# Recurrent unit of a hybrid backbone: branch products two tiles ahead, each convolution behind the gates of the tile in front

## The chip, the cores and the metric

The kernel runs on one core of a Trainium2 chip. Its five engines work side by side, each through its own queue in order: PE (TensorE, matrix products), ACT (ScalarE, functions), DVE (VectorE, elementwise work and scans), POOL (GpSimd) and SP (which here only issues DMAs). They wait for each other by semaphores. The metric is the time of one execution in microseconds (us), as the device measures it; the median of three runs is given.

## The reference

One inference step runs two trunk layers over 512 latent and 128 context tokens of width 1024. Layer 0 mixes tokens by neighbourhood attention, layer 1 by a bidirectional gated linear recurrent unit; behind each stands a SwiGLU feed-forward part. The change lies in layer 1's mixer:

```
def _rglru_coeffs(xc, w_a, b_a, w_i, b_i, lam):
    xb = xc.reshape(B, T, LRU_BLOCKS, LRU_BLOCK_W)
    r = sigmoid(einsum('btnk,nkj->btnj', xb, w_a).reshape(B, T, D) + b_a)
    i = sigmoid(einsum('btnk,nkj->btnj', xb, w_i).reshape(B, T, D) + b_i)
    log_a = -LRU_C * r * softplus(-lam)
    a = exp(log_a)
    b = sqrt(-expm1(2.0 * log_a)) * (i * xc)

def _lru_mixer(xm, h0, w_in, conv_w, conv_b, ...):
    gate, xr = jnp.split(xm @ w_in, 2, axis=-1)
    xc = _centred_depthwise_conv(xr, conv_w, conv_b)     # width 4
    # coefficients a, b for each direction; h_t = a_t * h_(t-1) + b_t
    y = (hs_f + hs_b) * gelu(gate)
    return y @ w_out, ...
```

Everything is float32.

## The kernel before

Tokens lie along the free dimension (640 columns: 512 latent, 128 context), features along the 128 partitions, so that a width of 1024 is eight tiles. Products with the large weights are done as three matmuls in a faster float format: weights and activations are each split into a high and a low part, and `some` (L214) multiplies high by high, high by low and low by high. A weight tile of 1024 x 128 is a unit: `unit` (L163) loads it twice in this stage, once by SP into `raw` (L167) and once by POOL straight into the high part `whi` (L178); DVE then makes the low part `wlo` as raw minus whi (L182). There are three buffers each of raw, whi and wlo.

The recurrent unit treats the eight tiles of its width one by one, in steps of the loop at L1438:

- `lru_xr` (L1242): the branch product of tile f, 24 matmuls (eight feature tiles, three each) over the first 384 columns and 24 over the other 256, copied by ACT (L1251) into `xr`. Two xr buffers.
- `lru_a` (L1254): loads the four 128 x 128 gate weights `gw` (SP, L1257); the convolution, one ACT step (L1259) and three DVE steps (L1261), into `xc`, two buffers; then four gate products (L1271, four float32 matmul records each) into `gp`, a PSUM tile with two buffers, each followed by a tanh on ACT (L1272); last a DVE step on the second pair (L1273), the last reader of xc.
- `lru_b` (L1276): coefficients; exp (L1283), tanh (L1284) and square root (L1285) on ACT, four DVE steps.
- `lru_c` (L1290): four scans and sums on DVE; POOL copies the last state of each direction (L1298).
- `lru_gate` (L1317): the product of the gate branch with its GELU (L1325, L1327).
- `lru_d` (L1307): the result times the gate, split for the output projection (L1313, L1315).

In step t of the loop the program asks for `lru_a` of tile t, the branch product of tile t+1, `lru_b` of tile t-1, `lru_c` of tile t-2, the gate branch of tile t-2 and `lru_d` of tile t-2. Ahead of the loop stand the branch products of tile 0 and half of tile 1 and the gate branch of tile 0, interleaved with the end of the stage before. The order in the program isn't the order on the engines: the kernel is built with a planner (`schedule_with_timeline_sim=True`, L1484) that lays the instructions into the five queues by a simulated timeline, with the program's order as the priority among those that are ready there. At run time each queue is in order.

Behind the unit comes the output projection (`project_halves`, L1463), which multiplies the first six tiles of its input in one pass and the last two in a second, and the last feed-forward part.

Of the kernel before, what the change touches and what calls it, by code (L numbers as in the profile page):

```python
# [9 lines left out]
F32 = mybir.dt.float32  # L10
# [5 lines left out]
P = 128  # L16
D = 1024
KT = D // P
# [15 lines left out]
LW = 643  # L34
# [91 lines left out]
class _Step:  # L126
# [1113 lines left out]
        return [lambda t0=t0, t1=t1, **kw: ev(t0, self.chunk(u, hi, lo, t0, t1, **kw)) for t0, t1 in CHL]  # L1240

    def lru_xr(self, f, hi, lo, after=None):  # L1242
        xr = self.xrs[f % 2]
        nat = xr[:, 2:514].rearrange("p (r c) -> p c r", r=ROWS)

        def ev(t0, ps):
            for o, a, b, r in ((nat[:, 56:64], 0, 64, ROWS), (nat[:, 0:40], 64, 384, ROWS),
                               (nat[:, 40:56], 384, 512, ROWS), (xr[:, 517:645], 512, 640, 0)):
                if t0 <= a and b <= t0 + 384:
                    v = ps[:, a - t0:b - t0]  # L1250
                    self.nc.scalar.copy(o, v.rearrange("p (c r) -> p c r", r=r) if r else v)  # L1251
        return self.halves(self.i["wi"][KT + f], hi, lo, ev, after)

    def lru_a(self, f, lp):  # L1254
        nc, xr = self.nc, self.xrs[f % 2]
        gw = self.t([P, 2, 2, P], F32, "gw", 2, lp)
        nc.sync.dma_start(gw, self.i["wg"][f])  # L1257
        xc = self.t([P, LW], F32, "xc", 2, lp)
        nc.scalar.activation(xc, xr[:, 0:LW], AF.Identity, scale=self.col("cw0", f), bias=self.col("cb", f))  # L1259
        for j in range(1, 4):  # L1260
            nc.vector.scalar_tensor_tensor(xc, xr[:, j:j + LW], self.col(f"cw{j}", f), xc, ALU.mult, ALU.add)  # L1261

        def lt():
            return self.t([P, 2, LW], F32, "lt", NLT, lp)
        tr, ti = lt(), lt()
        for w, tl in enumerate((tr, ti)):
            for d in range(2):
                c = (w * 2 + d) * KT + f
                ps = self.pp.tile([P, 1024], F32, tag="gp", name=self.nm("gp"), bufs=2)
                for s0, s1 in ((0, 512), (512, LW)):  # L1270
                    nc.tensor.matmul(ps[:, s0:s1], gw[:, w, d], xc[:, s0:s1], start=True, stop=True)  # L1271
                nc.scalar.activation(tl[:, d], ps[:, 0:LW], AF.Tanh, scale=0.5, bias=self.hb[:, c:c + 1])  # L1272
        nc.vector.scalar_tensor_tensor(ti, ti, 1.0, xc[:, None, :].broadcast_to([P, 2, LW]), ALU.add, ALU.mult)  # L1273
        return lt, tr, ti
# [63 lines left out]
    def run(self):  # L1338
        nc, tc, i, o = self.nc, self.tc, self.i, self.o
# [19 lines left out]
        xhi = self.big()  # L1359
        xlo = self.big()  # L1360
# [44 lines left out]
        xhi = self.big(n=NTOK + 2)  # L1405
        xlo = self.big(n=NTOK + 2)
# [12 lines left out]
        xhi, xlo = self.nh, self.nl  # L1419
# [2 lines left out]
        ylo = self.big()  # L1422
        with self.phase("lru", at=1) as lp:
            A, B, C, G = {}, {}, {}, {}
            self.xrs = [self.t([P, 648], F32, f"xr{j}", 1, lp) for j in range(2)]
            for xr in self.xrs:
                for a, b in ((0, 2), (514, 517), (645, 648)):
                    nc.gpsimd.memset(xr[:, a:b], 0.0)

            def gate(g, after=None):  # L1430
                G[g], halves = self.lru_gate(g, xhi, xlo, lp, after)
                return halves
            x0, g0, x1 = self.lru_xr(0, xhi, xlo), gate(0, self.sq), self.lru_xr(1, xhi, xlo, self.dg)
            x0[0](pins={3: self.at})
            g0[0](pins={0: self.rr})
            for step in (x1[0], x0[1], g0[1]):
                step()
            for t in range(KT + 2):  # L1438
                if t < KT:
                    A[t] = self.lru_a(t, lp)  # L1440
                if t + 1 < KT:
                    for step in self.lru_xr(t + 1, xhi, xlo) if t else x1[1:]:
                        step()
                if 0 < t <= KT:
                    B[t - 1] = self.lru_b(t - 1, *A.pop(t - 1))
                if t > 1:
                    C[t - 2] = self.lru_c(t - 2, *B.pop(t - 2))
                if t > 2:
                    for step in gate(t - 2):
                        step()  # L1450
                if t > 1:
                    self.lru_d(t - 2, C.pop(t - 2), G.pop(t - 2), yhi, ylo)
            nc.gpsimd.dma_start(o["nh"], self.st)
        x1, x2 = self.big(n=NTOK + 2), self.big(n=NTOK + 2)
# [33 lines left out]
```

## Time and profile before

| what | us |
|---|---|
| median of three runs | 1521.86 |
| lowest, highest | 1520.55, 1522.31 |
| the profiled execution | 1522.37 |
| its span in the profile | 1520.6 |
| gate products' matmuls (L1271) in the unit | from 875.29 to 991.3 |

The profile is of one execution. A timeline row gives an instruction's start, its length, its engine and line, what it writes and reads, and in brackets how long its engine had been idle and which instruction it waited for by the profile. An instruction that waits for several others is put down to the one that came last by the profile. Matmuls overlap in PE's pipeline, so the distance between two starts says more than a length. A row of windows gives the busy time of each engine in a stretch.

### The profile page before, as it was taken

To read this page: it belongs to the slowest core of one execution; us is meant where nothing else is said; L and a number is where in the kernel's file an instruction comes from. 1 tells how busy PE (TensorE), PEld (TensorE's weight loads), DVE (VectorE), ACT (ScalarE), POOL (GpSimd) and SP (SyncE) were. 2 spreads that over 40 slices of the span, in tenths; PEclk is the share of its full clock that TensorE was granted. 3 is DMA by queue.
4 is the path that set the end of the run, shared out by engine and by line. 5 is a ranking of instruction groups with operands and counts; after the bars stand their busy time and mean duration, and the time that the engine had idled before them with its cause. 6 is when DMAs were issued, how large, how long until landed. Compare 5 with 4: busy or idle time off the path is not lost. (4 is left out here: it accounts for less than half of the span.)

```text
span 1520.6 us, 26116 instructions
## 1 busy us (share of the span) xinstructions
PE 1491.2 (98%) x10373; PEld 1441.8 (95%) x10373; DVE 1061.5 (70%) x2005; ACT 698.1 (46%) x1268; POOL 261.4 (17%) x276
## 2 busy tenths in 40 slices
PE   8999999999999999999999999899999999999997
PEld 5999999889999999999999887799999999999997
DVE  5778998679999997434443769876975655566555
ACT  4676766654332123312321478764644342434243
POOL 0112132100111110000000014230232323222211
PEclk9999999999999999999999999999999999999999
DMA  9644665446556664222222543316242231323211
GB/s 375 174 143 160 186 189 167 117 139 194 176 185 195 207 196 132 62 84 84 65 73 83 150 134 102 119 59 216 70 156 80 74 111 57 100 67 97 71 56 70
DMA packets 72330, 196.65 MB, mean 129 GB/s; under 512 B 8048, under 2 KB 24592, under 8 KB 72080
## 3 DMA queue, kind: packets, MB, share of 16 engines
q1 hardware_dynamic: 57392, 142.32, 29.6%
q0 software_dynamic: 14240, 51.98, 11.1%
q8 instruction: 81, 1.33, 0.4%
q10 hardware_dynamic: 576, 0.68, 0.1%
q14 instruction: 41, 0.34, 0.1%
HBM read 179.48 MB, written 8.92 MB: 124 GB/s over the span
## 5 line engine op out<-in xcount | busy, mean ns | idle before, releaser
L221 PE MATMUL mm<-big,whi 128*128 128x320 f32 (+3 forms) x1233 | 383.9, 313 | 4.0 <-ACT big L1313 2.8
L222 PE MATMUL mm<-big,whi 128*128 128x320 f32 (+3 forms) x1233 | 384.2, 312 | 1.7 <-DVE big L1315 1.3
L223 PE MATMUL mm<-big,wlo 128*128 128x320 f32 (+3 forms) x1233 | 384.1, 312 | 0.2 <-DVE wlo L182 0.2
L221 PEld LDWEIGHTS mm<-big,whi 128*128 128x128 f32 x1233 | 233.0, 189 | 6.7 <-ACT big L1313 3.5
L222 PEld LDWEIGHTS mm<-big,whi 128*128 128x128 f32 x1233 | 233.6, 189 | 3.8 <-DVE big L1315 2.2
L223 PEld LDWEIGHTS mm<-big,wlo 128*128 128x128 f32 x1233 | 233.2, 189 | 1.6 <-DVE wlo L182 0.4
L250 DVE SCALAR_TENSOR_TENSOR mprod<-mraw,csb 128x1024 f32<-128x1024 f32 x160 | 194.9, 1218 | 11.8 <-DMA mraw<-in_wm 11.4
L590 DVE SCALAR_TENSOR_TENSOR x<-mm,G,x 128x320 f32<-128x320 f32 (+2 forms) x192 | 77.8, 435 | 82.4 <-PE mm L223 82.3
L180 ACT CAST whi<-raw 128x1024 fp32r<-128x1024 f32 (+1 forms) x71 | 73.9, 1041 | 113.9 <-PE mm L222 65.6
L182 DVE TENSOR_TENSOR wlo<-raw,whi 128x1024 fp32r<-128x1024 f32 (+1 forms) x87 | 105.9, 1218 | 28.7 <-ACT whi L180 16.5
L221 PE MATMUL mm<-big,whx 128*128 128x320 f32 (+3 forms) x348 | 108.4, 311 | 0.0
L223 PE MATMUL mm<-big,wlx 128*128 128x320 f32 (+3 forms) x348 | 108.0, 310 | 0.0
L222 PE MATMUL mm<-big,whx 128*128 128x320 f32 (+3 forms) x348 | 107.9, 310 | 0.0
L246 POOL DMA_DIRECT2D mraw<-in_wm x80 | 43.0, 537 | 358.6 <-DVE mprod L250 266.0
L221 PE MATMUL mx<-big,whi 128*128 128x320 f32 (+3 forms) x287 | 89.5, 312 | 0.0
L223 PE MATMUL mx<-big,wlo 128*128 128x320 f32 (+3 forms) x287 | 88.9, 310 | 0.0
L222 PE MATMUL mx<-big,whi 128*128 128x320 f32 (+3 forms) x287 | 88.7, 309 | 0.0
L221 PE MATMUL mx<-big,whx 128*128 128x320 f32 (+3 forms) x260 | 80.6, 310 | 0.0
L223 PE MATMUL mx<-big,wlx 128*128 128x320 f32 (+3 forms) x260 | 80.5, 310 | 0.0
L180 ACT CAST whx<-raw 128x1024 fp32r<-128x1024 f32 (+1 forms) x40 | 41.1, 1029 | 85.9 <-PE mm L222 47.3
L222 PE MATMUL mx<-big,whx 128*128 128x320 f32 (+3 forms) x260 | 80.3, 309 | 0.0
L1313 ACT CAST whi<-raw 128x1024 fp32r<-128x1024 f32 (+1 forms) x41 | 41.3, 1008 | 70.3 <-PE mm L222 45.2
(347 smaller groups left out, 3725.3 us busy)
## 6 DMA issues: line engine op xcount, KB each, us to landing
raw<-in_gu SPq DMA_DIRECT2D x88, 512.0 KB, 3.5
mraw<-in_wm POOLq DMA_DIRECT2D x80, 512.0 KB, 3.9
raw<-in_dn SPq DMA_DIRECT2D x24, 512.0 KB, 3.6
sw<-in_wm SPq DMA_DIRECT2D x16, 512.0 KB, 10.7
raw<-in_wqk SPq DMA_DIRECT2D x16, 512.0 KB, 4.8
raw<-in_wi SPq DMA_DIRECT2D x16, 512.0 KB, 3.5
whi<-in_wi POOLq DMA_DIRECT2D x16, 512.0 KB, 3.9
raw<-in_dn SPq DMA_DIRECT2D x16, 448.0 KB, 3.3
```

The costliest lines, as they stand in the source:

```text
L180: nc.scalar.copy(hi, raw)
L182: nc.vector.tensor_tensor(lo, raw, hi.bitcast(F32), ALU.subtract)
L221: nc.tensor.matmul(ps, hi[:, k], xhi[:, k, s], start=(k == 0), stop=False)
L222: nc.tensor.matmul(ps, hi[:, k], xlo[:, k, s], start=False, stop=False)
L223: self.done = nc.tensor.matmul(ps, lo[:, k], xhi[:, k, s], start=False, stop=(k == last)).ins
L246: nc.gpsimd.dma_start(w, self.i["wm"][l * 6 + j - 2, f])
L250: nc.vector.scalar_tensor_tensor(prod, w, 1.0, self.csb[:, s], ALU.mult, ALU.mult, accum_out=out[:, s, f:f + 1])
L590: self.nc.vector.scalar_tensor_tensor(xs, ps[:, a - t0:b - t0], G[:, s, f:f + 1], xs, ALU.mult, ALU.add)
L1313: self.nc.scalar.copy(hi, v)
```

## The change

The branch product runs two tiles ahead of the gates in place of one, and a tile's convolution becomes a function of its own, called right behind `lru_a` of the tile in front. xr and xc get a third buffer each. The second half of tile 1's branch product, which stood behind `lru_a` of tile 0 in the first step, stays there. The rest of the step keeps its order.

```diff
     def lru_xr(self, f, hi, lo, after=None):
-        xr = self.xrs[f % 2]
+        xr = self.xrs[f % 3]
...
-    def lru_a(self, f, lp):
-        nc, xr = self.nc, self.xrs[f % 2]
-        gw = self.t([P, 2, 2, P], F32, "gw", 2, lp)
-        nc.sync.dma_start(gw, self.i["wg"][f])
-        xc = self.t([P, LW], F32, "xc", 2, lp)
+    def lru_conv(self, f, lp):
+        nc, xr = self.nc, self.xrs[f % 3]
+        xc = self.t([P, LW], F32, "xc", 3, lp)
         nc.scalar.activation(xc, xr[:, 0:LW], AF.Identity, scale=self.col("cw0", f), bias=self.col("cb", f))
         for j in range(1, 4):
             nc.vector.scalar_tensor_tensor(xc, xr[:, j:j + LW], self.col(f"cw{j}", f), xc, ALU.mult, ALU.add)
+        return xc
+
+    def lru_a(self, f, lp, xc):
+        nc = self.nc
+        gw = self.t([P, 2, 2, P], F32, "gw", 2, lp)
+        nc.sync.dma_start(gw, self.i["wg"][f])
...
-            self.xrs = [self.t([P, 648], F32, f"xr{j}", 1, lp) for j in range(2)]
+            self.xrs = [self.t([P, 648], F32, f"xr{j}", 1, lp) for j in range(3)]
...
+            xc = self.lru_conv(0, lp)
             for t in range(KT + 2):
                 if t < KT:
-                    A[t] = self.lru_a(t, lp)
+                    A[t] = self.lru_a(t, lp, xc)
+                if t == 0:
+                    x1[1]()
                 if t + 1 < KT:
-                    for step in self.lru_xr(t + 1, xhi, xlo) if t else x1[1:]:
+                    xc = self.lru_conv(t + 1, lp)
+                if t + 2 < KT:
+                    for step in self.lru_xr(t + 2, xhi, xlo):
                         step()
                 if 0 < t <= KT:
                     B[t - 1] = self.lru_b(t - 1, *A.pop(t - 1))
```

## The prediction

> **What bounds the kernel now.** I read the page's table of engines first, then the busy time by windows, and from there PE's own timeline in the stretch that the edit touches.
>
> ```profile
> span 1520.6 us, 26116 instructions
> PE 1491.2 (98%) x10373; PEld 1441.8 (95%) x10373; DVE 1061.5 (70%) x2005; ACT 698.1 (46%) x1268; POOL 261.4 (17%) x276
> ```
>
> PE is busy for 98% of the span. A change that leaves PE's instructions alone, as this one does, can only gain what PE loses by waiting. The recurrent unit lies between about 862 and 1002 us. In the rows below the columns are PE, PEld, DVE, ACT and POOL busy with their counts, then the granted clock, the DMA share and GB/s.
>
> ```profile
> 862.00:1002.00 140.00, 133.26 (x779) 115.23 (x778) 105.24 (x121) 109.33 (x152) 37.35 (x25) 0.98 0.37 113
> 905.00:955.00 50.00, 48.02 (x270) 41.00 (x269) 48.36 (x59) 43.64 (x61) 23.05 (x11) 0.97 0.35 105
> 910.00:920.00 10.00, 8.14 (x42) 5.95 (x40) 10.00 (x12) 7.45 (x10) 10.00 (x2) 0.89 0.37 107
> 960.00:970.00 10.00, 8.26 (x50) 7.11 (x49) 10.00 (x11) 6.00 (x9) 0.00 (x0) 1.00 0.36 105
> 980.00:990.00 10.00, 8.30 (x31) 6.30 (x32) 9.97 (x11) 5.30 (x7) 1.45 (x3) 0.83 0.34 108
> ```
>
> PE is idle for 140.00 - 133.26 = 6.7 us of this stage, nearly all of it in three windows; DVE and ACT have 35 and 31 us of room there, but hardly any from 905 to 955 us (DVE 48.36 of 50). The PE timeline names the waits (start, length, instruction, idle time and releaser):
>
> ```profile
> 917.48 2.29 PE L1271 MATMUL gp<-xc,gw 128*128 128x512 f32 x4 [1.86 <-ACT lt L1272]
> ...
> 965.96 2.43 PE L1271 MATMUL gp<-xc,gw 128*128 128x512 f32 x8 [1.74 <-DVE xc L1261]
> ...
> 981.70 3.75 PE L1271 MATMUL gp<-xc,gw 128*128 128x512 f32 x8 [2.16 <-ACT lt L1285]
> 985.10 0.67 PE L221 MATMUL mm<-big,whi 128*128 128x384 f32 x1
> ...
> 1024.47 0.41 PE L221 MATMUL mm<-big,whi 128*128 128x320 f32 x1 [1.57 <-ACT big L1313]
> ```
>
> The first three stand at gate products (L1271), the fourth just behind the stage, where the output projection waits for the last two tiles. What released the second and third is read from DVE's timeline:
>
> ```profile
> 955.36 0.27 DVE L1304 TENSOR_TENSOR lt<-lt 128x128 f32<-128x128 f32 x1
> 959.47 1.23 DVE L182 TENSOR_TENSOR wlo<-raw,whi 128x1024 fp32r<-128x1024 f32 x1 [3.83 <-PE mm L223]
> 960.61 0.88 DVE L1261 SCALAR_TENSOR_TENSOR xc<-xr,cols,xc 128x643 f32<-128x643 f32 x1
> ...
> 965.02 0.88 DVE L1261 SCALAR_TENSOR_TENSOR xc<-xr,cols,xc 128x643 f32<-128x643 f32 x1
> ...
> 979.57 1.23 DVE L182 TENSOR_TENSOR wlo<-raw,whi 128x1024 fp32r<-128x1024 f32 x1 [2.85 <-PE mm L223]
> 980.71 0.88 DVE L1261 SCALAR_TENSOR_TENSOR xc<-xr,cols,xc 128x643 f32<-128x643 f32 x1
> ```
>
> The last convolution step of tile 6 ends at 965.90 and PE starts at 965.96; that of tile 7 ends at 981.59 and PE starts at 981.70. So the third wait, put down to L1285, is also one for xc. Both times a weight difference (L182) stood idle at the head of DVE's queue with convolution steps behind it. POOL's timeline shows what it waited for:
>
> ```profile
> 952.16 3.52 POOL L1298 COPY st<-lt 128x1 f32<-128x1 f32 x1 [10.99 <-DVE lt L1296]
> 955.62 0.53 POOL L178 DMA_DIRECT2D whi<-in_wi  x1
> ...
> 973.05 2.79 POOL L1298 COPY st<-lt 128x1 f32<-128x1 f32 x1 [0.47 <-DVE lt L1296]
> 975.78 0.53 POOL L178 DMA_DIRECT2D whi<-in_wi  x1
> ...
> DMA to landing us min/median/max: 3.7/3.9/5.0
> ```
>
> 955.62 + 3.8 = 959.4 and 975.78 + 3.8 = 979.6: the landings of whi fit the starts of L182 better than the PE matmuls named. The chain is: state copy on POOL, weight load behind it, weight difference on DVE, convolution behind that, gate products on PE.
>
> **The change part by part.** *Convolution and branch products earlier.* The counts stay: 8 ACT and 24 DVE convolution steps, 8 branch products, 8 gw loads. Only places change. These rows show where the convolutions stand now (ACT):
>
> ```profile
> 913.40 0.93 ACT L1259 ACTIVATE xc<-xr,cols 128x643 f32<-128x643 f32 x1 [0.80 <-DVE lt L1273]
> ...
> 916.63 1.48 ACT L1272 ACTIVATE lt<-gp,l_hb 128x643 f32<-128x643 f32 x2
> ...
> 953.79 0.49 ACT L1251 COPY xr<-mm 128x128 f32<-128x128 f32 x2
> ...
> 970.35 0.49 ACT L1251 COPY xr<-mm 128x128 f32<-128x128 f32 x2 [0.94 <-PE mm L223]
> 970.88 0.93 ACT L1259 ACTIVATE xc<-xr,cols 128x643 f32<-128x643 f32 x1
> ```
>
> ```profile
> 875.29 2.33 PE L1271 MATMUL gp<-xc,gw 128*128 128x512 f32 x8
> 877.37 0.41 PE L221 MATMUL mm<-big,whi 128*128 128x384 f32 x1
> 877.62 0.34 PE L222 MATMUL mm<-big,whi 128*128 128x384 f32 x1
> 877.80 0.34 PE L223 MATMUL mm<-big,wlo 128*128 128x384 f32 x1
> ```
>
> Tile 7's branch is copied out at 970.35, its convolution follows, and its gate products start at 981.70: 11 us for work that passes two in-order queues. A product of one tile is 24 matmuls of 384 columns at 0.18 us between starts and 24 of 256, two thirds of that: 24 x 0.18 x 1.67 = 7.2 us. In the new order the branch product of tiles 5 to 7 moves ahead of one gate-branch product, so xr is there about 7 us sooner: 963 for tile 7 and 947 for tile 6. The convolution, now ahead of the previous tile's coefficients and of the scan before those, needs 0.93 + 3 x 0.88 = 3.6 us, and even with the 3.83 us stall of L182 in front it ends by about 971 and 955, 10 us before PE asks. Both waits go: 1.74 + 2.16 = 3.90 us.
>
> The third wait drags a slow clock along. From 981.70 to 985.10 the eight gate matmuls take 3.40 us, where eight of them take 877.37 - 875.29 = 2.08: 1.32 us. The window from 980 shows a granted clock of 0.83, which is 3.4 us at half. With the wait this goes too: 3.90 + 1.32 = **5.2 us**.
>
> The Trainium skill's page "TensorE: Matmul & The Clock Gate", section "HAM oscillation — how this bites in real kernels", asks only that PE have no gaps over about 3.4 us. By it, 2.16 us costs nothing more, and the gain would be 3.9 us; the trace disagrees, since the clock fell to 0.89 and 0.83 in the windows of the 1.86 us and 2.16 us waits, and I go by the rows.
>
> *What is late next.* The wait at 917 is ACT's: gate products need a gp buffer that the tanh frees, and that tanh starts only at 916.63, behind a convolution that waited 0.80 us for L1273 to free xc, and behind other work. The third xc buffer takes the 0.80 away, and the convolution is off that place, but the stretch has DVE and ACT full. Bounds for this wait: gone (-1.86, and about as much clock as above) or unchanged; I take unchanged, since tanh work isn't less. The wait at 1024 hangs on the tail of DVE (second rival); I take it as unchanged too.
>
> *DMA queues.* On SP the gw load now follows the convolution's ACT and DVE steps, which are not in its queue; x(t+2)'s raw load goes ahead of what belongs to older tiles. On POOL the whi load of x(t+2) keeps its place behind the state copies. The three weight buffers turn over in PE's order as before, so I count nothing; third rival if wrong.
>
> *Memory.* One more xr and xc is (648 + 643) x 4 B = 5.2 KB per partition, and three memsets more.
>
> ```profile
> 851.84 0.26 POOL L1428 MEMSET xr<- 128x2 f32 x6
> 866.05 0.57 POOL L178 DMA_DIRECT2D whi<-in_wi  x1 [13.96 <-PE mm L223]
> ...
> 861.59 0.80 SPq L1257 DMA_DIRECT2D gw<-in_wg  x2
> ```
>
> Three memsets cost 0.13 us inside POOL's 13.96 us of idling. If the new buffer lies over a tile of the stage before, as gw does whose load left at 861.59, it waits until about then: hidden too, since POOL's next work is at 866.05. What lies over this pool afterwards shifts as well; nearest row for a loss is that of 1.57 us at the stage's end, above: between -1.6 and +1.6, taken as 0.
>
> Span: 1520.6 - 5.2 = 1515.4. The profiled execution took 1522.37 us, 1.8 more than its span, and 0.5 more than the median of the runs. So the median goes from 1521.86 to **1516.7 us**.
>
> **Rivals.**
>
> *All four waits go.* With xc always ahead, the 917 wait and its slow clock (1.86 + 1.3) and the 1024 wait (1.57) go too: 1516.7 - 4.7 = 1512.0. For it: 35 us of room on DVE. Against it: none of that room lies between 905 and 955.
>
> *The tail takes the gain.* Behind the stage the output projection needs the last two tiles, and DVE works without a break up to them:
>
> ```profile
> 1005.51 2.91 DVE L1286 SCALAR_TENSOR_TENSOR lt<-lt,lt 128x1286 f32<-128x1286 f32 x2 [1.76 <-ACT lt L1285]
> ...
> 1024.45 1.56 DVE L1315 TENSOR_TENSOR big<-lt,big 128x640 fp32r<-128x640 f32 x2
> ```
>
> If DVE ends at 1026 as now, PE waits there 5.2 us longer and the time is 1521.9: no change. Against it: DVE idled before 1005.51, waiting for ACT, whose input is tile 7's gates; these come sooner by the waits removed. Or the planner places the convolutions as before: same time.
>
> *Weight loads starve.* Two products are 14.4 us of PE; a load needs 3.9 us and L182 1.2, so it may leave 9.3 us late. The state copies held POOL up to this long:
>
> ```profile
> 910.03 12.52 POOL L1298 COPY st<-lt 128x1 f32<-128x1 f32 x1
> ```
>
> That would cost 3.2 us and a slow clock of 1.3 each time: one takes the gain to 0.7 us (1521.2). The Trainium skill's page "SBUF — State Buffer", section "Who interferes with whom", says that a GpSimd instruction that reads SBUF is blocked by a DVE one with two SBUF inputs; DVE was busy for the whole of 910 to 920, so the trace bears this out. Against it: the holds at 952 and 973 delayed loads without starving PE.
>
> *ACT becomes the bound: slower.* With xc ready early, gate products are issued early, and each pair fills the two gp buffers until ACT has done its tanh; PE, in order, stands behind them, as it did at 917. Its price there was 1.86 us and some 1.3 of clock, 3.2. Before, xc's lateness kept the other tiles from it. One such stall more leaves 1519.9, two 1523.1, three 1526.3: slower from two on. For it: ACT is 87% busy from 905 to 955. Against it: per tile ACT and DVE have less work than PE (109 and 105 against 133 us over the stage).
>
> **How the numbers follow.** Chances: forecast 0.45, all four 0.13, tail or no effect 0.17, weight loads 0.07, ACT 0.18 (1525). A measurement of this kernel tells about 0.2%, 3 us, from no change, so faster means under 1518.8: 0.45 + 0.13 = 0.58; same 0.24; slower 0.18. The range takes in the first two cases, the no-change ones and the milder half of the last: 1511 to 1524.
>
> **What would show it.** Right: no PE wait on L1261 or at a gate product near 965 and 981; the last L1261 of tiles 6 and 7 ending 5 us or more before their first L1271; a granted clock of 1.00 there; the output projection starting about 5 us sooner. The tail: an L1313 wait grown from 1.57 to 6 us. ACT: several waits like that at 917, with L1272 as releaser. Starving: PE waits on L182. Wrong altogether: L1261 still last ahead of L1271.

## The result, and the profile after

| kernel | median us | lowest to highest | runs |
|---|---|---|---|
| before | 1520.41 | 1515.12 to 1524.14 | 20 |
| changed | 1524.32 | 1519.58 to 1528.22 | 20 |

The ratio is 1.0026, with a 95% interval from 1.0016 to 1.0036. The changed kernel is slower by 0.26%, 3.9 us. The single executions of either kernel lie up to 9 us apart; their standard deviation is 2.5 us for the changed kernel and 2.6 for the one before.

The profiled execution of the changed kernel took 1525.4 us. The page's span and table of engines, and then the windows of the recurrent unit (columns as in the prediction):

```profile
span 1523.6 us, 26120 instructions
PE 1492.2 (98%) x10373; PEld 1443.4 (95%) x10373; DVE 1061.1 (70%) x2005; ACT 697.6 (46%) x1268; POOL 260.9 (17%) x279
```

```profile
862.00:1002.00 140.00, 129.32 (x738) 111.45 (x737) 103.31 (x117) 104.89 (x144) 38.79 (x25) 0.95 0.36 111
905.00:955.00 50.00, 48.56 (x290) 42.60 (x290) 43.11 (x51) 38.31 (x53) 27.52 (x11) 1.00 0.36 111
960.00:970.00 10.00, 5.63 (x25) 5.59 (x26) 5.82 (x6) 9.94 (x15) 0.06 (x1) 0.66 0.35 111
990.00:1000.00 10.00, 8.56 (x36) 6.49 (x37) 9.91 (x13) 9.07 (x13) 2.88 (x2) 0.66 0.16 53
```

The work is the same (10373 matmuls). In the unit PE is now idle for 140.00 - 129.32 = 10.7 us, where it was 6.7, and the mean clock fell from 0.98 to 0.95. ACT and DVE are less busy than before in the same 140 us (104.89 and 103.31 against 109.33 and 105.24): neither has more to do, so something stands still. PE's timeline names where:

```profile
915.14 1.35 PE L1275 MATMUL gp<-xc,gw 128*128 128x512 f32 x4 [1.44 <-ACT lt L1276]
...
964.37 0.58 PE L221 MATMUL mm<-big,whi 128*128 128x256 f32 x1 [5.37 <-ACT xr L1251]
...
969.65 2.45 PE L1275 MATMUL gp<-xc,gw 128*128 128x512 f32 x8
...
991.44 2.51 PE L1275 MATMUL gp<-xc,gw 128*128 128x512 f32 x4 [3.49 <-ACT lt L1276]
...
996.96 0.39 PE L221 MATMUL mm<-big,whi 128*128 128x256 f32 x1
```

The two waits for xc, near 965 and 981, are gone, and so is the one behind the stage at 1024. Two longer ones have come: 5.37 us for ACT's copy of a branch product out of PSUM (L1251), and 3.49 us for a tanh (L1276). Both waits are for ACT, so ACT's timeline is next:

```profile
943.97 0.52 ACT L1331 ACTIVATE gl<-gl 128x384 f32<-128x384 f32 x1
...
945.61 0.80 ACT L1276 ACTIVATE lt<-gp,l_hb 128x643 f32<-128x643 f32 x1 [0.22 <-PE gp L1275]
957.63 0.73 ACT L1317 CAST big<-lt 128x640 fp32r<-128x640 f32 x1 [11.22 <-DVE lt L1312]
958.26 0.80 ACT L1276 ACTIVATE lt<-gp,l_hb 128x643 f32<-128x643 f32 x1
...
963.51 0.81 ACT L1251 COPY xr<-mm 128x64 f32<-128x64 f32 x2
...
977.41 0.73 ACT L1317 CAST big<-lt 128x640 fp32r<-128x640 f32 x1 [4.47 <-DVE lt L1312]
...
990.59 0.80 ACT L1276 ACTIVATE lt<-gp,l_hb 128x643 f32<-128x643 f32 x1
```

ACT stands idle for 11.22 us at a cast (L1317, the split of a tile's result in `lru_d`), with the tanh of the next gates, two exps and the xr copies queued behind it. PE waits 5.37 us of that. The 3.49 us wait stands behind a second stop of this kind: the cast at 977.41 was idle for 4.47 us, ACT then works without a gap, and the tanh that PE needs starts only at 990.59. The first cast waits for DVE's multiply of the result with the gate (L1312). DVE's timeline, columns as above:

```profile
937.52 1.23 DVE L182 TENSOR_TENSOR wlo<-raw,whi 128x1024 fp32r<-128x1024 f32 x1 [3.88 <-issue]
...
944.92 0.29 DVE L1308 TENSOR_TENSOR lt<-lt 128x128 f32<-128x128 f32 x1
...
950.44 1.22 DVE L182 TENSOR_TENSOR wlo<-raw,whi 128x1024 fp32r<-128x1024 f32 x1 [3.02 <-PE gp L1275]
...
953.79 1.28 DVE L1300 TENSOR_TENSOR_SCAN lt<-lt,cols,lt 128x512 f32<-128x512 f32 x1
...
956.48 0.40 DVE L1300 TENSOR_TENSOR_SCAN lt<-lt,lt 128x128 f32<-128x128 f32 x1
956.79 0.80 DVE L1312 TENSOR_TENSOR lt<-lt,gl 128x640 f32<-128x640 f32 x1
957.51 0.88 DVE L1259 SCALAR_TENSOR_TENSOR xc<-xr,cols,xc 128x643 f32<-128x643 f32 x1
```

The multiply's input from ACT, the GELU (L1331), was done at 943.97 + 0.52 = 944.49, and its input from DVE, the last sum of the tile's scans (L1308), at 945.21. The multiply ran only at 956.79, 11.6 us later. It stands in DVE's queue behind the four scans of the next tile (953.79 to 956.79 between starts, 3.0 us), behind a weight difference that was idle for 3.02 us, and behind other steps of later tiles. The idle time of 3.88 us ahead of the earlier weight difference had already made DVE late as a whole. The same tile in the kernel before, ACT's rows and then DVE's:

```profile
943.96 0.52 ACT L1327 ACTIVATE gl<-gl 128x384 f32<-128x384 f32 x1
947.27 0.73 ACT L1313 CAST big<-lt 128x640 fp32r<-128x640 f32 x1 [2.79 <-DVE lt L1308]
```

```profile
946.37 0.87 DVE L1308 TENSOR_TENSOR lt<-lt,gl 128x640 f32<-128x640 f32 x1
...
950.38 1.33 DVE L1296 TENSOR_TENSOR_SCAN lt<-lt,cols,lt 128x512 f32<-128x512 f32 x1
```

There the GELU was done at the same time, 944.48, and the multiply ran 1.9 us after it, ahead of the scans. So at run time it's the multiply's place in DVE's queue, and not a later GELU, that holds the cast. Last, POOL of the changed kernel shows what the two weight differences waited for:

```profile
922.37 11.32 POOL L1302 COPY st<-lt 128x1 f32<-128x1 f32 x1 [0.47 <-DVE lt L1300]
933.63 0.53 POOL L178 DMA_DIRECT2D whi<-in_wi  x1
941.12 1.02 POOL L1302 COPY st<-lt 128x1 f32<-128x1 f32 x1 [6.97 <-DVE lt L1300]
942.61 4.05 POOL L1302 COPY st<-lt 128x1 f32<-128x1 f32 x1 [0.47 <-DVE lt L1300]
946.60 1.06 POOL L178 DMA_DIRECT2D whi<-in_wi  x2
```

933.63 + 3.8 = 937.4 and 946.60 + 3.8 = 950.4: the landings of whi, as in the kernel before.

The profiled spans differ by 1523.6 - 1520.6 = 3.0 us. PE's idle time in the unit makes +3.9, the slow clock behind the waits about +1.7, and the vanished wait of the window from 1002 to 1030 about -1.6: +4.0. The remaining -1.0 isn't explained further (at 862 us this execution was already some eight matmuls ahead). The clock's part is worked out like this. Behind 964.37, 24 matmuls of 256 columns take 969.65 - 964.37 = 5.28 us, where 0.12 us between starts makes 2.9. Behind 991.44, eight gate matmuls and five of 256 columns take 996.96 - 991.44 = 5.52 us, where 2.08 + 5 x 0.12 makes 2.7. That is 5.2 us. In the kernel before it was some 3.5: about 1.8 behind 917, and about 1.7 behind 981.70, where the eight gate matmuls lost 1.32 and the three matmuls behind them, up to 986.12, some 0.4 more.

### The profile page after: what moved, and what is told of

Same layout as the page of the kernel before. It is cut to its first block, busy times and chain, and to the rows that moved or that the text cites. A ratio compares the mean times of both kernels' runs of the same rounds, so it can differ in the third digit from the quotient of the medians.

```text
span 1523.6 us, 26120 instructions
## 1 busy us (share of the span) xinstructions
PE 1492.2 (98%) x10373; PEld 1443.4 (95%) x10373; DVE 1061.1 (70%) x2005; ACT 697.6 (46%) x1268; POOL 260.9 (17%) x279
## 5 line engine op out<-in xcount | busy, mean ns | idle before, releaser
L223 PE MATMUL mm<-big,wlo 128*128 128x320 f32 (+3 forms) x1233 | 383.8, 312 | 0.2 <-DVE wlo L182 0.2
L223 PEld LDWEIGHTS mm<-big,wlo 128*128 128x128 f32 x1233 | 233.6, 190 | 1.4 <-DVE wlo L182 0.4
L250 DVE SCALAR_TENSOR_TENSOR mprod<-mraw,csb 128x1024 f32<-128x1024 f32 x160 | 195.2, 1220 | 11.4 <-DMA mraw<-in_wm 10.9
L182 DVE TENSOR_TENSOR wlo<-raw,whi 128x1024 fp32r<-128x1024 f32 (+1 forms) x87 | 106.1, 1220 | 27.5 <-ACT whi L180 15.6
L223 PE MATMUL mm<-big,wlx 128*128 128x320 f32 (+3 forms) x348 | 108.0, 310 | 0.0
L223 PE MATMUL mx<-big,wlo 128*128 128x320 f32 (+3 forms) x287 | 88.8, 310 | 0.0
L180 ACT CAST whx<-raw 128x1024 fp32r<-128x1024 f32 (+1 forms) x40 | 41.1, 1030 | 86.7 <-PE mm L222 48.0
L223 PE MATMUL mx<-big,wlx 128*128 128x320 f32 (+3 forms) x260 | 80.5, 310 | 0.0
L1317 ACT CAST whi<-raw 128x1024 fp32r<-128x1024 f32 (+1 forms) x41 | 41.3, 1008 | 71.7 <-PE mm L222 44.7
```

The costliest lines, as they stand in the source:

```text
L180: nc.scalar.copy(hi, raw)
L182: nc.vector.tensor_tensor(lo, raw, hi.bitcast(F32), ALU.subtract)
L223: self.done = nc.tensor.matmul(ps, lo[:, k], xhi[:, k, s], start=False, stop=(k == last)).ins
L250: nc.vector.scalar_tensor_tensor(prod, w, 1.0, self.csb[:, s], ALU.mult, ALU.mult, accum_out=out[:, s, f:f + 1])
L1317: self.nc.scalar.copy(hi, v)
```

## The experiments

**Two theories.** The first, *order*: the branch product that goes ahead pushes the gate branch's product back one place; GELU, multiply and cast follow later in the plan, the multiply lands behind the next tile's scans, and the cast blocks ACT. The second, *holds*: the one-element state copies on POOL hold weight loads at random, L182 blocks DVE, and the changed kernel merely had worse draws. A third, that the early convolution itself crowds ACT or DVE, was tried first. All ratios are to runs of the kernel before on the same chip in the same session; they are not quotients of the medians shown. Each has its 95% interval.

**1. The convolution early, the branch products one ahead.** Against the changed kernel:

```diff
+                if 0 < t < KT - 1:
+                    for step in self.lru_xr(t + 1, xhi, xlo):
+                        step()
                 if t + 1 < KT:
                     xc = self.lru_conv(t + 1, lp)
-                if t + 2 < KT:
-                    for step in self.lru_xr(t + 2, xhi, xlo):
-                        step()
```

> The kernel before with the convolution called right behind the gates of the tile in front and a third xr and xc, but the branch product one tile ahead as before. Built, its five queues hold the instructions of the kernel before in the same places but for six neighbours. Theory (the slowdown comes from the branch product going ahead of the gate branch, not from the convolution's place): same time as before within 2 us, the PE waits near 965 and 981 us there as before. Rival (the early convolution takes DVE time from the chain that PE needs, or the shifted memory adds waits): slower by 3 to 4 us, like the changed kernel.

Measured: 1518.13 us median, ratio 0.9996 [0.9984, 1.0009]. The place of the convolution in the program costs and brings nothing that can be told from zero. The kernel has the third xr and xc too, so the shifted memory isn't the cause either. Of the two PE waits that were expected as before, its trace has one, 2.26 us at 977.01. The planner's five queues say the same without a run: with the branch products two ahead and the convolution left in `lru_a`, they are those of the changed kernel, instruction for instruction. Here the planner placed the convolution when its input was there, wherever the program asked for it. So the change consists of the branch products alone.

**2 and 3. No state copies for tiles 0 to 6**, in the changed kernel and in the one before:

```diff
-            nc.gpsimd.tensor_copy(st, h[:, d, e:e + 1])
+            if f == 7:
+                nc.gpsimd.tensor_copy(st, h[:, d, e:e + 1])
...
+        nc.vector.memset(self.st, 0.0)
```

> The changed kernel without the state copies of tiles 0 to 6 on POOL (that part of the state output is left at zero); all other queues keep their order. Theory (ACT stands 11.2 us at the cast of tile 2's result because its multiply is queued on DVE behind the next tile's scans, and DVE itself came late by about 3 to 7 us since weight loads stood behind state copies on POOL): the L182 waits of 3.9 and 3.0 us near 937 and 950 go, the ACT idle time shrinks from 11.2 to about 5 to 8 us, the PE wait near 964 from 5.4 to 0 to 3 us; 3 to 5 us faster than the changed kernel, some PE wait at 991 is left. Rival (the held weight loads alone are the cause): both PE waits go altogether with their slow clock, 10 us or more faster. Rival (the queue order alone is the cause): waits and time as in the changed kernel, within 1 us.

> The kernel before without the state copies of tiles 0 to 6 on POOL (that part of the state output is left at zero); all other queues keep their order. If the chain read from the profile of before is right (state copy on POOL, weight load behind it, L182, convolution, gate products), the L182 waits near 959 and 979 us shrink from 3.8 and 2.9 to under 1 us, the PE waits of 1.7 and 2.2 us near 965 and 981 go, and the kernel is 3 to 5 us faster than before. Rival (L182 waited for PE's use of the weight buffer, as the profile names it): waits and time unchanged within 1 us.

Measured: the changed kernel without the copies 1518.76 us, ratio 1.0001 [0.9989, 1.0013]; the kernel before without them 1517.00, 0.9986 [0.9972, 1.0000]. The groups by line from 900 to 1002 us show the effect; the last column is the idle time ahead of the group, with its releasers. First the changed kernel, then the same without copies, then the kernel before without copies:

```profile
L182 DVE TENSOR_TENSOR wlo<-raw,whi 128x1024 fp32r<-128x1024 f32 x8 | 9.8, 1228 | 6.9 <-issue 3.9 <-PE gp L1275 3.0
L1317 ACT CAST big<-lt 128x640 fp32r<-128x640 f32 x5 | 3.6, 726 | 17.5 <-DVE lt L1312 17.5
```

```profile
L182 DVE TENSOR_TENSOR wlo<-raw,whi 128x1024 fp32r<-128x1024 f32 x9 | 11.3, 1250 | 1.3 <-ACT whi L180 1.3
L1318 ACT CAST big<-lt 128x640 fp32r<-128x640 f32 x5 | 3.6, 727 | 10.9 <-DVE lt L1313 10.9
```

```profile
L182 DVE TENSOR_TENSOR wlo<-raw,whi 128x1024 fp32r<-128x1024 f32 x9 | 11.0, 1222 | 3.1 <-ACT whi L180 3.1
L1314 ACT CAST big<-lt 128x640 fp32r<-128x640 f32 x5 | 3.6, 725 | 4.1 <-DVE lt L1309 4.1
```

Without the copies no weight difference waits for a landing in this stretch: the chain that the prediction read is real, and holds are part of the loss. They cost the changed kernel 1.0026 - 1.0001 = 0.25%, 3.8 us, and the one before 0.14%, 2.1 us. The two PE waits near 965 and 981 went from the kernel before as expected, but the gain is below the 3 to 5 us that were expected. And with the copies gone the casts of the changed kernel still stand idle for 10.9 us in total, against 4.1. Its PE wait of 5.37 us is gone with the longest stop of ACT, but the one of 3.49 us stays:

```profile
PE gp L1275 <- ACT lt L1276: 6.2, 4, 3.5
```

(us in total, times, longest.) What is left between the two, 1.0001 - 0.9986 = 0.15%, 2.3 us, is the order. The intervals of these two overlap, so the next runs test it by itself.

**4 and 5. The multiply ahead of the scans.** The scans of tiles 3 to 5 are pinned to be issued behind the multiply of the tile in front, with the state copies (4) and without (5):

```diff
-                nc.vector.tensor_tensor_scan(hv, av, hv, init, ALU.mult, ALU.add)
+                with self.pin(self.mul if f in (3, 4, 5) else None):
+                    nc.vector.tensor_tensor_scan(hv, av, hv, init, ALU.mult, ALU.add)
...
-        self.nc.vector.tensor_tensor(y, y, G, ALU.mult)
+        self.mul = self.nc.vector.tensor_tensor(y, y, G, ALU.mult).ins
```

> The changed kernel with the scans of tiles 3, 4 and 5 held on DVE behind the multiply (L1312 in the changed kernel) of the tile in front of them. Theory: ACT's idle time at the cast of tiles 2 and 3 shrinks from 11.2 and 4.5 us by the 3.0 us of the scans each and more, the PE waits near 964 and 991 us (5.4 and 3.5 us) shrink to under 2 us each, and the time falls by 4 to 8 us against the changed kernel. Rival (the place of the multiply is not what ACT's delay comes from): waits and time within 1.5 us of the changed kernel, or the wait moves to DVE standing at the multiply for the gate's GELU.

> The kernel of e4 (scans of tiles 3 to 5 behind the multiply of the tile in front) without the state copies of tiles 0 to 6 (that part of the state output is left at zero); all other queues keep the order of e4. Theory (two causes that add: the queue order, with ACT standing at a cast, and the random holds of POOL): faster than e2 by 3 to 5 us, so 1513 to 1516 us, no ACT wait of over 3 us at a cast between 930 and 975, spread of the runs under 2 us. Rival (the order of multiply and scans does nothing on its own, e4's profiled run was a lucky one): 1517 to 1520 us like e2, with a PE wait of 3 us or more near 980.

Measured: with copies 1519.09 us, 1.0008 [0.9992, 1.0025], its executions between 1513.34 and 1526.39; without 1516.26, 0.9979 [0.9965, 0.9992]. Between runs 2 and 5, which have no such copies, the pin takes 0.22%, 3.3 us. The groups and PE's waits of run 5:

```profile
L1319 ACT CAST big<-lt 128x640 fp32r<-128x640 f32 x6 | 4.4, 726 | 6.4 <-DVE lt L1314 6.4
```

```profile
PE gp L1275 <- ACT lt L1276: 3.5, 3, 1.9
```

The cast's idle time fell from 10.9 to 6.4 us and the wait of 3.5 us is gone: the place of one multiply on DVE did make PE wait for a tanh on ACT. With copies the gain is 1.0026 - 1.0008 = 0.18%, 2.7 us, less than the 4 to 8 us expected, and the intervals overlap.

**6 and 7. The state copies on VectorE**, a complete kernel: 6 is the changed kernel so, 7 has the pin of 4 as well.

```diff
-            nc.gpsimd.tensor_copy(st, h[:, d, e:e + 1])
+            nc.vector.tensor_copy(st, h[:, d, e:e + 1])
```

> The changed kernel with the 16 state copies on DVE in place of POOL; complete output. If the holds on POOL are what the removal in e2 took away, this is as fast as e2: 1518 to 1520 us, 4 to 6 us faster than the changed kernel, with a narrow spread (standard deviation under 2 us against 2.5). Rival (leaving the copies out helped in some other way, or 16 more steps on a full DVE cost as much): 1522 us or more.

> The kernel of e4 with the state copies on DVE; complete output. Theory: as e5 plus at most 1 us for the copies, 1513 to 1517 us, and so 3 to 7 us faster than before. Rival as in e5: 1518 us or more.

Measured: 1520.07 us, 1.0007 [0.9996, 1.0018], and 1516.03, 0.9984 [0.9973, 0.9995]. Moving the copies takes 1.0026 - 1.0007 = 0.19%, 2.9 us, about as much as leaving them out (0.25%) but less than the 4 to 6 us expected; they cost DVE 0.14 us each. The pin takes 1.0007 - 0.9984 = 0.23%, 3.5 us, in two complete kernels of one session, as between runs 2 and 5. Run 7 is 2.4 us faster than the kernel before, where 3 to 7 were expected.

**8 and 9. The gate branch ahead of the branch product.** If the loss is that the gate product was passed, letting it go first must take the loss away and keep the gain. 8 has the copies on VectorE, 9 on POOL.

```diff
+                if t > 2:
+                    for step in gate(t - 2):
+                        step()
                 if t + 2 < KT:
                     for step in self.lru_xr(t + 2, xhi, xlo):
                         step()
...
-                if t > 2:
-                    for step in gate(t - 2):
-                        step()
```

> The changed kernel with the gate branch asked for ahead of the branch product in each step, and the state copies on DVE; complete output. Theory (the branch product ahead of the gate branch makes the GELU, the multiply behind it and ACT's cast late): the multiplies stand ahead of the scans, ACT's waits at the casts fall below 3 us, PE waits at gate products below 2 us, 1513 to 1517 us. Rival (branch two ahead is slow wherever the gate branch stands, since tanh, exp and copies bunch up on ACT): 1519 us or more, PE waits of 3 us with L1276 as releaser.

> The kernel of e8 with the state copies on POOL as in the changed kernel: the order of gate branch and branch product alone. Theory of two causes that add: the order is worth what separates e8 from e6 (ratio 0.9964 against 1.0007, some 6 us), the copies some 3 us, so this kernel stands between: 1515 to 1518 us, ratio 0.997 to 0.999, with a wider spread (standard deviation over 2 us). Rival (the holds cost nothing once nothing is queued behind late multiplies): 1513 to 1514 us like e8. Rival (order alone does nothing): 1522 us or more, like the changed kernel.

Measured: 8 took 1513.36 us, 0.9964 [0.9949, 0.9979], and is faster than both kernels; 9 took 1517.89, 0.9987 [0.9973, 1.0000]. Against the changed kernel's order that is 1.0007 - 0.9964 = 0.43% with the copies on VectorE and 1.0026 - 0.9987 = 0.39% on POOL, 6.5 and 5.9 us, from the place of one product. Against the kernel before, run 9 gains 0.13%, 2.0 us, and its interval just reaches zero. Both runs lie where they were expected. Groups by line, window and PE's waits of run 8:

```profile
L182 DVE TENSOR_TENSOR wlo<-raw,whi 128x1024 fp32r<-128x1024 f32 x10 | 12.1, 1213 | 0.1
L1317 ACT CAST big<-lt 128x640 fp32r<-128x640 f32 x6 | 4.3, 719 | 0.6 <-DVE lt L1312 0.6
L1302 DVE COPY st<-lt 128x1 f32<-128x1 f32 x12 | 1.7, 140 | 0.0
```

```profile
862.00:1002.00 140.00, 137.68 (x834) 121.35 (x833) 112.62 (x136) 117.42 (x160) 6.91 (x13) 1.00 0.36 114
```

```profile
PE mm L221 <- ACT big L1317: 1.9, 1, 1.9
PE gp L1275 <- ACT lt L1276: 1.7, 2, 1.5
```

The cast's idle time is 0.6 us and L182's 0.1. PE is idle for 2.3 us in the unit at a clock of 1.00. The wait behind the stage, for the last casts (1.9), stays.

**10. The copies on VectorE in the kernel before.** The same one-line edit as in 6.

> The kernel before with the state copies on DVE; complete output; the planner moves some steps of tiles 5 to 7 with it. Theory: like e3, ratio 0.997 to 0.9995, so e8's 0.9964 needs the branch two ahead as well. Rival (all of e8's gain comes from the copies): 0.9964 or less.

Measured: 1525.56 us, 1.0037 [1.0023, 1.0052]. It is slower and not faster, against both expectations. PE's waits, ACT's timeline and one row of DVE's:

```profile
PE mm L221 <- ACT big L1313: 8.0, 1, 8.0
```

```profile
983.47 0.72 ACT L1313 CAST big<-lt 128x640 fp32r<-128x640 f32 x1 [6.14 <-DVE lt L1308]
...
986.10 1.49 ACT L1272 ACTIVATE lt<-gp,l_hb 128x643 f32<-128x643 f32 x2
...
1023.40 1.46 ACT L1313 CAST big<-lt 128x640 fp32r<-128x640 f32 x2 [12.02 <-DVE lt L1308]
```

```profile
982.64 0.79 DVE L1308 TENSOR_TENSOR lt<-lt,gl 128x640 f32<-128x640 f32 x1
```

The planner lays the whole stage anew. On DVE the multiply of tile 4 (982.64) now stands behind the four scans of tile 5 (from 979.63), and ACT stands idle for 6.14 us at its cast: the same trap as in the changed kernel, in the old order of products. In ACT's queue the planner put the tanh of tile 7 behind that cast and a second gate branch, so it starts at 986.10, where it started at 980.32 in run 3. The last casts came at 1023.40 in place of 1017.16, and PE waited 8.0 us for them, at the place that the rival of the tail named. So the copies on VectorE aren't worth something fixed. Their worth is that of the plan which comes out.

## Why the prediction was wrong

Its direction was wrong: it said 1516.7 us in a range of 1511 to 1524, and 1524.32 came, just past the top end and slower than before.

**The bound and the forecast waits: right.** In the unit, PE's waits and the slow clock behind them moved the time. Tile 6's last convolution step ends at 957.51 + 0.88 = 958.39 and its gate products start at 969.65; tile 7's ends at 978.18, 3.0 us ahead of its gate products at 981.14. No PE wait on xc is left. The convolution's place was of no account (run 1), only the branch product's.

**The chain through POOL and L182: right in kind, too large in size.** Run 3 takes the state copies away, and with them the two L182 waits and both forecast PE waits of the kernel before. That is worth 2.1 us on average, with an interval from 0 to 4.3, where the profiled execution showed 5.2 at two places. That execution was one draw from a spread of several microseconds, and the prediction took it for the mean. Run 9, which has the branch products two ahead but doesn't let them pass the gate branch, gains 2.0 us.

**The step that failed** is this one: "the branch product of tiles 5 to 7 moves ahead of one gate-branch product, so xr is there about 7 us sooner". The branch products did come sooner (tile 7's copy at 964.93 in place of 970.35). But the step counts who gains and not who is passed, and so the sum puts the price of passing at nothing. The gate-branch product comes 7.2 us of PE work later in the queue, and in the plan GELU, multiply and cast follow it. In the traces, the GELU of the tile shown was done at the same time in both kernels; the multiply's place behind the scans is what the changed plan left. The trace doesn't show the planner's simulated time, so how exactly the plan came to put the multiply behind the scans is inferred; that this place costs 3.3 us is shown by the pin (run 5 against 2, and 3.5 us by run 7 against 6), and that passing the gate product costs some 6 us by runs 8 and 9. Split at run 9, the measured loss of 3.9 us is 2.0 us gained by the branch products' earlier place and 5.9 us lost by the passing. The prediction followed the loads through the queues that the product moved past, but not the consumers of the product that it overtook.

**The wait at 917 and the tail.** The first was taken as unchanged and came to 1.44 in place of 1.86 us. The second was taken as unchanged and went: PE came to that place only at 1026.82, when the first of the two casts (from 1026.03) was done.

**The weight loads.** The whi load "keeps its place behind the state copies", the prediction said, and counted nothing for it. PE hardly waited for a weight (0.2 us at L223), so the rival of starving loads fell as it was put. But the loads were held as before. The changed kernel gained 3.8 us without the holds and the kernel before 2.1; that its order is hurt more, since scans, multiply and so ACT hang on DVE's queue behind L182, fits this but isn't shown, as the intervals are wider than the difference.

**The rival of a bound ACT** foresaw the side and the sign, several PE waits released by the tanh, but not the cause. ACT did less work in the stage, not more (104.89 against 109.33 us), and stood idle at a cast while the tanh waited behind it. Its chance of 0.18 was for another mechanism, and that its 1525 us lies so close to the measured time is luck.

## What to carry to other kernels

When a product is moved ahead of another, price both sides: list what the overtaken product feeds on every in-order queue, and look for an instruction that would stand at the head of its queue waiting for it (here a cast on ACT, 11.22 us). Where the profile names a wait for an engine that is less busy than before, read that engine's own idle time first. Where single executions spread by several microseconds, a wait's length in one trace is a draw and not its cost, and where a planner lays out the queues, a small edit has to be read in the queues that come out (in run 10 the move of a few tiny copies brought the same trap back).

## What the runs showed of the hardware

**Tiny copies on POOL widen the spread.** The copies of one element per partition (L1302) took 1.02, 4.05 and 11.32 us in the rows above. One and the same copy, the second of the unit, took 12.52 us in the kernel before, 6.59 in the changed one and 12.51 in run 9. The group from 900 to 1002 us of the changed kernel:

```profile
L1302 POOL COPY st<-lt 128x1 f32<-128x1 f32 x12 | 32.1, 2672 | 52.8 <-DVE lt L1300 49.0 <-ACT lt L1276 3.3 <-ACT lt L1287 0.5
```

Twelve took 32.1 us; on DVE twelve took 1.7 us (run 8). Without them on POOL the standard deviation of the executions was 1.3 to 1.7 us (runs 2, 3, 5 to 8 and 10); with them it was 2.6 and 2.5 in the kernels before and after, and 1.9, 3.9 and 2.4 in runs 1, 4 and 9. That fits the rule of the Trainium skill's page "SBUF — State Buffer", section "Who interferes with whom", that the prediction named. But a busy DVE alone doesn't make a hold: the copy at 941.12 took 1.02 us beside DVE's scans. No run held DVE's inputs apart, so the cause of a single hold wasn't isolated.

**The slow clock doesn't follow from the length of one wait.** The 5.37 and 3.49 us waits were each followed by matmuls at about half speed (256 columns each 0.21 us between starts, where 0.12 is usual). So were waits of 1.86 us (kernel before, at 917) and 1.85 (run 3, at 916.90, its window from 910 to 920 us at a clock of 0.86). But run 5 waited 1.87 us at the same kind of product and went on at full speed, as did runs 4, 7 and 10 behind 1.88, 1.87 and 1.88 us:

```profile
982.12 1.35 PE L1275 MATMUL gp<-xc,gw 128*128 128x512 f32 x4 [1.87 <-ACT lt L1276]
```

What decides between the two at this length was not settled.
